# Sixty-eight weight tiles at distances of their own, and every other pair read backward

## The chip, the cores and the metric

The kernel runs on one core of one Trainium2 chip. The metric is the device time of one launch in microseconds (us): 628.13 us before the change, the median of three runs from 628.09 to 628.43. TensorE does the products (PE in the profile, PEld for its weight loads), VectorE (DVE) and ScalarE (ACT) prepare operands and drain results, GpSimd (POOL) and SyncE (SP) mostly issue DMAs.

## The reference

One transformer-like layer on a (512, 1024) input in float32. The change touches the input projection of the gated MLP alone, the second line below:

```python
h = layer_norm(ALPHA * h + mixed @ w_out[l], ln1_g[l], ln1_b[l])
a, u = jnp.split(h @ w_ffn_in[l], 2, axis=-1)      # w_ffn_in: (1024, 2 * 2816)
a = causal_dwconv(a, conv_w[l], conv_b[l])
f = (jax.nn.gelu(a, approximate=False) * u) @ w_ffn_out[l]
h = layer_norm(ALPHA * h + f, ln2_g[l], ln2_b[l])
```

## The kernel before, in words

Everything is kept transposed: channels on the 128 partitions, the 512 tokens along the free dimension. Each float32 operand is split into a high part (`split`, L71: a rounding copy to float32r on ScalarE, L75) and a low part (the rest, on VectorE, L76), and one float32 product is three float32r matmuls, high by high, high by low, low by high (`mm3`, L240, whose matmuls stand on L242, L245 and L246). In each, a 128 x 128 block of weights is loaded as the stationary operand and the activations are the moving operand.

The FFN input has 22 pairs of 128 output channels (one for `a`, one for `u`). Pairs 2 to 18 (`SEVEN`, 17 of them) are computed with Strassen-like products of seven, on blocks of half the channels by half the tokens, so their moving operand has 256 columns. A pair has four combined weight tiles: A, X and Y of 128 x 1024 and D of 128 x 512. `s_mm` (L271) multiplies half a tile (four blocks) with one of the block combinations of h: A twice, X twice, Y twice, D once. So a pair takes 7 x 4 x 3 = 84 matmuls, and the 17 pairs take 1428. Of these 24 fall to each A, X and Y and 12 to each D. The products go into halves of PSUM banks: `ba` and `bc` in `seven_a` (L277), `bb` in `seven` (L284); in the profile their names are saf, scf and sbf (sai and sag and so on for the same scheme in the first projections). The pairs 0, 1 and 19 to 21 are done plainly (`fi_mm`, L879).

The high and low weight tiles live in rings of five slots each (`slot`, L122), tags `whi` and `wlo`. A slot is `SLOT = D + 64` float32 wide, 4352 bytes in a partition, which is 17 x 256. In the built program both rings, and all the wide activation tiles that TensorE reads beside them (hT_hi, hT_lo, the combinations T3, T4, nT1, nT2, xT, zT, sd), start at 192 mod 256 bytes of the partition. So the distance of a weight block from the moving operand, mod 256, is the offset of the tile in its slot: `BESIDE = 2` elements, 8 bytes, for all products of seven and for the four plain tiles of pairs 0 and 1 (`near`), and 0 bytes for all others.

The order of the work on each engine is fixed by a scheduler when the program is built. TensorE runs ahead through banks and slots, and the ring of weight tiles is filled `LEAD = 3` tiles ahead (`weights`, L235; `fetch`, L129; `fetch_seven`, L193, which forms the combined weights and calls `slot` on L207).

Of the kernel before, what the change touches and what calls it, by code (L numbers as in the profile page):

```python
# [34 lines left out]
BESIDE = 2  # L35
# [7 lines left out]
SEVEN = tuple(range(2, 19))  # L43
# [8 lines left out]
def layer_kernel(ctx: ExitStack, tc: tile.TileContext, xT, x, w_v, w_c, rel_bias, invcnt, w_group,  # L52
# [14 lines left out]
    def flip(v):  # L67
        (pst, pn), (_, n) = v.ap
        return bass.AP(tensor=v.tensor, offset=v.offset + P - 1, ap=[[pst, pn], [P, n // P], [-1, P]])

    def split(hi, lo, src, copy=None):  # L71
        if copy:
            copy(hi, src)
        else:
            state["hi"] = nc.scalar.activation(hi, src, AF.Copy)  # L75
        state["lo"] = nc.vector.tensor_tensor(lo, src, hi.bitcast(F32), op=ALU.subtract)  # L76
        return state["lo"]
# [41 lines left out]
    ready = {}  # L119


    def slot(i, n, near=False):  # L122
        o = BESIDE if near else 0
        return tuple(wp.tile([P, SLOT], F32R, tag=f"w{q}", name=f"w{q}{i}", bufs=RING)[:, o:o + n]
                     for q in ("hi", "lo"))

# [2 lines left out]
    def fetch(pool=None, early=None):  # L129
# [17 lines left out]
        if isinstance(chunks[i], tuple):  # L147
            ready[i] = (fetch_fo if i >= FO0 else fetch_seven)(i, *chunks[i])
            return
        raw = wp.tile([P, D], F32, tag="wraw", name=f"wraw{i}", bufs=3)  # L150
        if pool is None:
            hi, lo = slot(i, D, FI0 <= i < FI0 + COVER)
        else:
            hi = pool.tile([P, D], F32R, name=f"whi{i}")
            lo = pool.tile([P, D], F32R, name=f"wlo{i}")
        parts = 2 if early else 1
        for c in range(parts):
            sl = slice(c * (D // parts), (c + 1) * (D // parts))
            (nc.scalar if early else nc.sync).dma_start(raw[:, sl], chunks[i][:, sl])
            split(hi[:, sl], lo[:, sl], raw[:, sl])  # L160
            if c == 0 and early:
                state["w0"] = raw[:, sl]
                early()
# [29 lines left out]
    def fetch_seven(i, key, q):  # L193
        n = S if q == "D" else D
        raw = raws[key, "A" if q == "Y" else q]
        if q == "X" and key in SUMMED:
            with tc.issue_after(state["Y"].ins):
                for c, o in ((slice(S, D), raws[key, "D"]), (slice(0, S), raws[key, "A"][:, :S])):
                    nc.vector.tensor_tensor(raw[:, c], raw[:, :S], o, op=ALU.add)
        if q == "Y":  # L200
            with ExitStack() as held:
                if key == ("f", COVER // 2):
                    held.enter_context(tc.issue_after(state["h"].ins))

                for c, o in ((slice(0, S), raws[key, "X"][:, S:]), (slice(S, D), raw[:, :S])):
                    nc.vector.tensor_tensor(raw[:, c], o, raw[:, c], op=ALU.add)
        hi, lo = slot(i, n, True)  # L207
        state[q] = split(hi, lo, raw)
        return hi, lo

# [6 lines left out]
    def fetch_fo(i, name, c):  # L217
        sl = piece(c)
        n = sl.stop - sl.start
        step = {"T3": "=B11", "B11": "+B12", "T1": "+B22", "T2": "+B21", "T4": None}  # L220
        if name in step:
            raw = tw[:, sl]
        else:
            raw = wp.tile([P, D], F32, tag="wraw", name=f"wraw{i}", bufs=3)[:, :n]
            nc.sync.dma_start(raw, half(name, sl))
        hi, lo = slot(i, n)
        split(hi, lo, raw)
        then = step.get(name)
        if then and then[0] == "+":
            nc.gpsimd.dma_start(raw, half(then[1:], sl), accum_op=ALU.add)  # L230
        elif then:
            nc.sync.dma_start(raw, half(then[1:], sl))
        return hi, lo

    def weights(i):  # L235
        while state["next"] <= min(i + LEAD, state["limit"]):
            fetch()
        return ready[i]

    def mm3(out_, w, a, start, stop, pin=False, **kw):  # L240
        (wh, wl), (ah, al) = w, a
        ins = nc.tensor.matmul(out_, wh, ah, start=start, stop=False, **kw)  # L242
        if pin:
            tc.keep_in_program_order(ins)
        nc.tensor.matmul(out_, wh, al, start=False, stop=False, **kw)  # L245
        nc.tensor.matmul(out_, wl, ah, start=False, stop=stop, **kw)  # L246

    def split3(v, a):
        return tuple(t.rearrange("p (a c) -> p a c", a=a) for t in v)
# [20 lines left out]

    def s_mm(key, q, part, act_, b, start, pin=False):  # L271
        wh, wl = split3(weights(at[(*key, q)]), 4 if q == "D" else KT)
        for k in range(4):
            mm3(b, (wh[:, 4 * part + k, :], wl[:, 4 * part + k, :]), (act_[0][:, k, :], act_[1][:, k, :]),
                start and k == 0, k == 3, pin and k == 0, skip_group_check=not start)

    def seven_a(key, whole, y):  # L277
        ba, bc = (bank(f"s{q}{key[0]}{key[1]}") for q in "ac")
        s_mm(key, "A", 0, (whole[0][:, k1, t1], whole[1][:, k1, t1]), ba[:, 256:], True)
        nc.scalar.activation(y, ba[:, 256:], AF.Copy)  # L280
        s_mm(key, "A", 1, (whole[0][:, k2, t1], whole[1][:, k2, t1]), bc[:, :256], True)
        return ba, bc

    def seven(key, whole, tt, y, u, done, between=None, begun=None):  # L284
        ba, bc = begun or seven_a(key, whole, y)
        bb = bank(f"sb{key[0]}{key[1]}")
        chain, low, c11 = ba[:, 256:], bb[:, :256], bc[:, :256]

        def b_(k, t):
            return whole[0][:, k, t], whole[1][:, k, t]  # L290

        flush()
        s_mm(key, "X", 0, tt["T3"], low, True)
        nc.scalar.activation(u[:, t2], low, AF.Copy)
        s_mm(key, "Y", 0, tt["nT2"], chain, False)
        nc.scalar.activation(u[:, t1], chain, AF.Copy)
        s_mm(key, "D", 0, tt["T4"], low, False)
        nc.vector.tensor_tensor(u[:, t1], u[:, t1], low, op=ALU.add)
        if between:
            between()  # L300
        s_mm(key, "X", 1, tt["nT1"], chain, False, between)
        nc.vector.tensor_tensor(u[:, t2], u[:, t2], chain, op=ALU.add)
        state["add"] = nc.vector.tensor_tensor(ba[:, t1], y, c11, op=ALU.add)

        def close():
            s_mm(key, "Y", 1, b_(k2, t2), chain, False, between)
            done(ba, u)

        pending.append(close)
# [93 lines left out]
    for kt in range(KT):  # L403
        wh, wl = split3(weights(kt // 2), 2)
        wh, wl = wh[:, kt % 2, :], wl[:, kt % 2, :]
# [197 lines left out]
    ap = attn.enter_context(tc.tile_pool(name="ap", bufs=2, reuse_waits="tile"))  # L603
# [72 lines left out]
    def br_mm(f, br, b=None, ks=range(4), pin=False):  # L676
        wh, wl = split3(weights(at["br", f]), KT)
        b = b or bank(f"br{f}_{br}")
        for k in ks:
            src = (zT_hi[:, k, :], zT_lo[:, k, :]) if br else (oT_hi[:, k, :], oT_lo[:, k, :])  # L680
            mm3(b, (wh[:, 4 * br + k, :], wl[:, 4 * br + k, :]), src, k == 0, k == 3, pin and k == ks[0])
        return b
# [7 lines left out]
    for f in range(KT - 1):  # L690
# [4 lines left out]
        for br in (1, 0):  # L695
            b = br_mm(f, br)
            if f < GSEVEN:
                t = gslot[8 * br + f]
                nc.vector.tensor_tensor(t, t, b, op=ALU.mult)
            else:  # L700
                t = branch[f, br] = unused.pop(0)
# [11 lines left out]
    def gate_done(f, ba, u):  # L713
        if f < KT - 1:
            for br, v, scale in ((0, ba, 1.0), (1, u, -1.0)):
                nc.scalar.activation(v, v, AF.Sigmoid, scale=scale)
                nc.vector.tensor_tensor(branch[f, br], branch[f, br], v, op=ALU.mult)
            merged(f, branch[f, 0], branch[f, 1])
        else:
            for br, v, scale in ((0, ba, 1.0), (1, u, -1.0)):  # L720
                gslot[8 * br + f] = unused.pop(0)
                nc.scalar.activation(gslot[8 * br + f], v, AF.Sigmoid, scale=scale)
# [6 lines left out]
    for f in range(GSEVEN, KT):  # L729
        if f == KT - 1:  # L730
# [3 lines left out]
              lambda ba, u, f=f: gate_done(f, ba, u), first_half if f == KT - 1 else None)  # L734
# [427 lines left out]
```

## Time and profile before

| | |
|---|---|
| median of the runs | 628.13 us |
| the profiled execution, from first to last instruction | 625.9 us |
| PE busy | 616.0 us, 98% |
| PEld busy | 552.9 us, 88% |
| DVE busy | 505.2 us, 81% |
| ACT busy | 353.8 us, 57% |

The span is that of one profiled execution, and lies 2.2 us under the median of the runs; times read from the trace are differences within it. In this profile the end of a matmul is modelled and matmuls overlap, so neither the mean duration of one (278 ns for 256 columns) nor the busy share tells how fast they follow each other. That is read from the starts: two rows of the timeline, and the number of matmuls between them.

### The profile page before, as it was taken

How to read it: one execution, taken by the hardware profiler on the slowest of the kernel's cores; microseconds unless marked ns; L12 is line 12 of the kernel's file. 1: busy time of each engine (PE TensorE's matmuls, PEld its weight loads, DVE VectorE, ACT ScalarE, POOL GpSimd, SP SyncE). 2: the span in 40 equal slices, each digit the busy share in tenths (PEclk: the TensorE clock that was granted, in tenths of full speed). 3: DMA queues.
4: the chain of work that ended last, by engine and by line, in shares of the span. 5: the costliest groups of instructions: out<-in, count | busy, mean ns of one | idle time of the engine just before them, and what ended most of it. 6: DMA issues, size and time to landing. Idle time of an engine off the chain costs nothing.

```text
span 625.9 us, 10417 instructions
## 1 busy us (share of the span) xinstructions
PE 616.0 (98%) x3988; PEld 552.9 (88%) x3988; DVE 505.2 (81%) x780; ACT 353.8 (57%) x536; POOL 119.0 (19%) x131
## 2 busy tenths in 40 slices
PE   8999999999999999999999999999999999999994
PEld 6899998777788998889999999999999888888884
DVE  6978787776494788399998988898988869798886
ACT  6646777655644567125566565566656346555442
POOL 0133134323132101110110101101100302123302
PEclk9999999999999999999999999999999999999998
DMA  9566647422548515816668687687745996899805
GB/s 321 163 193 187 177 121 223 134 78 78 169 111 211 149 60 177 293 43 225 146 167 208 184 201 185 176 201 201 187 97 161 325 254 127 221 192 207 195 1 134
DMA packets 40545, 107.70 MB, mean 172 GB/s; under 512 B 4384, under 2 KB 4648, under 8 KB 40240
## 3 DMA queue, kind: packets, MB, share of 16 engines
q1 hardware_dynamic: 27264, 71.90, 34.8%
q0 software_dynamic: 12656, 34.10, 28.0%
q10 hardware_dynamic: 576, 1.05, 0.5%
q8 instruction: 31, 0.51, 0.4%
q14 instruction: 18, 0.15, 0.1%
HBM read 102.82 MB, written 3.17 MB: 169 GB/s over the span
## 4 chain that ended last, share of the span: by engine, by line
PE 98%; DVE 1%; DMA 1%; DVEq 0%; issue 0%
PE saf L242 5%; PE saf L245 5%; PE saf L246 5%; PE v L420 3%; PE fi L242 3%; PE fi L245 3%; PE fi L246 3%; PE sbf L242 3%; PE sbf L246 3%; PE sbf L245 2%; PE br L242 2%; PE g L242 2%; PE g L246 2%; PE g L245 2%; PE wo L242 2%; PE br L246 2%
## 5 line engine op out<-in xcount | busy, mean ns | idle before, releaser
L75 ACT ACTIVATE whi<-wraw 128x1024 fp32r<-128x1024 f32 (+1 forms) x53 | 53.8, 1023 | 39.6 <-DMA wraw<-in_w_fo 8.1
L76 DVE TENSOR_TENSOR wlo<-wraw,whi 128x1024 fp32r<-128x1024 f32 (+1 forms) x53 | 65.1, 1235 | 12.7 <-ACT whi L75 12.5
L76 DVE TENSOR_TENSOR wlo<-araw,whi 128x1024 fp32r<-128x1024 f32 x52 | 63.3, 1225 | 9.4 <-ACT whi L75 9.1
L75 ACT ACTIVATE whi<-araw 128x1024 fp32r<-128x1024 f32 x52 | 54.4, 1058 | 20.2 <-PE saf L245 5.6
L189 POOL DMA_DIRECT2D xraw<-in_w_fi x15 | 18.0, 1203 | 135.9 <-DMA xraw<-in_w_fi 69.2
L75 ACT ACTIVATE whi<-tw 128x1024 fp32r<-128x1024 f32 (+1 forms) x30 | 29.5, 983 | 25.4 <-DMA tw<-in_w_fo 10.7
L76 DVE TENSOR_TENSOR wlo<-tw,whi 128x1024 fp32r<-128x1024 f32 (+1 forms) x30 | 33.5, 1129 | 9.0 <-ACT whi L75 9.0
L242 PE MATMUL sbf<-T_hi,whi 128*128 128x256 f32 x136 | 37.9, 279 | 0.0
L242 PE MATMUL saf<-hT_hi,whi 128*128 128x256 f32 x136 | 37.9, 279 | 0.0
L242 PE MATMUL saf<-nT_hi,whi 128*128 128x256 f32 x136 | 37.8, 278 | 0.0
L245 PE MATMUL saf<-hT_lo,whi 128*128 128x256 f32 x136 | 37.8, 278 | 0.0
L246 PE MATMUL saf<-nT_hi,wlo 128*128 128x256 f32 x136 | 37.8, 278 | 0.0
L246 PE MATMUL sbf<-T_hi,wlo 128*128 128x256 f32 x136 | 37.7, 278 | 0.0
L245 PE MATMUL sbf<-T_lo,whi 128*128 128x256 f32 x136 | 37.7, 277 | 0.0
L245 PE MATMUL saf<-nT_lo,whi 128*128 128x256 f32 x136 | 37.7, 277 | 0.0
L246 PE MATMUL saf<-hT_hi,wlo 128*128 128x256 f32 x136 | 37.6, 277 | 0.0
L245 PE MATMUL fi<-hT_lo,whi 128*128 128x256 f32 (+1 forms) x112 | 36.2, 326 | 0.0
L246 PE MATMUL fi<-hT_hi,wlo 128*128 128x256 f32 (+1 forms) x112 | 36.2, 325 | 0.0
L242 PE MATMUL fi<-hT_hi,whi 128*128 128x256 f32 (+1 forms) x112 | 36.1, 327 | 0.0
L560 POOL TENSOR_SCALAR pp<-pp,rs 128x128 f32<-128x128 f32 (+3 forms) x32 | 25.2, 803 | 36.7 <-DVE rs L557 26.6
L230 POOL DMA_DIRECT2D tw<-in_w_fo x18 | 15.6, 896 | 61.4 <-DVE wlo L76 61.4
L555 ACT ACTIVATE pp<-pp,nm 128x128 f32<-128x128 f32 (+3 forms) x32 | 17.6, 551 | 14.8 <-DVE nm L552 14.8
(346 smaller groups left out, 2171.8 us busy)
## 6 DMA issues: line engine op xcount, KB each, us to landing
tw<-in_w_fo POOLq DMA_DIRECT2D x20, 512.0 KB, 8.1
araw<-in_w_fi SPq DMA_DIRECT2D x17, 512.0 KB, 3.9
xraw<-in_w_fi SPq DMA_DIRECT2D x15, 512.0 KB, 4.3
xraw<-in_w_fi POOLq DMA_DIRECT2D x15, 512.0 KB, 6.2
wraw<-in_w_c SPq DMA_DIRECT2D x10, 512.0 KB, 4.4
wraw<-in_w_fi SPq DMA_DIRECT2D x10, 512.0 KB, 3.7
wraw<-in_w_fo SPq DMA_DIRECT2D x10, 512.0 KB, 5.1
tw<-in_w_fo SPq DMA_DIRECT2D x10, 512.0 KB, 7.5
```

The costliest lines, as they stand in the source:

```text
L75: state["hi"] = nc.scalar.activation(hi, src, AF.Copy)
L76: state["lo"] = nc.vector.tensor_tensor(lo, src, hi.bitcast(F32), op=ALU.subtract)
L189: state["acc"] = nc.gpsimd.dma_start(v, bass.AP(tensor=a.tensor, offset=a.offset, ap=[[pst, pn], [u.offset + S - a.offset, 2], [est, S]]), ...
L230: nc.gpsimd.dma_start(raw, half(then[1:], sl), accum_op=ALU.add)
L242: ins = nc.tensor.matmul(out_, wh, ah, start=start, stop=False, **kw)
L245: nc.tensor.matmul(out_, wh, al, start=False, stop=False, **kw)
L246: nc.tensor.matmul(out_, wl, ah, start=False, stop=stop, **kw)
L420: ins = nc.tensor.matmul(bs[j], xs_[j][a], (wh, wl)[b], start=kt == 0 and n == 0, stop=False)
L555: exps[h] = nc.scalar.activation(pp[:, offs[i]:offs[i] + n], pp[:, offs[i]:offs[i] + n], AF.Exp, bias=nm[:, i:i + 1], accum_out=rs[:, i:i ...
L560: nc.gpsimd.tensor_scalar(pp[:, offs[i]:offs[i] + n], pp[:, offs[i]:offs[i] + n], rs[:, i:i + 1], 1.0, op0=ALU.mult, op1=ALU.mult)
```

## The change

Each of the 68 weight tiles of the 17 pairs gets an offset of its own in its slot (the same in the high and the low ring), in place of 2 elements for all. Among the nine even pairs the 36 tiles get 0, 2, 4 ... 62 elements (0, 8, 16 ... 248 bytes) and the last four 1, 3, 5 and 7 elements (4, 12, 20, 28 bytes); among the eight odd pairs the 32 tiles get 0, 2, 4 ... 62 elements. For the odd pairs the moving operand is read backward, from the last of its 256 columns to the first, and the PSUM output is written backward too, so each result lands where it did. What is computed, and all other tiles, stay as they were.

```diff
+    def back(v):
+        (pst, pn), (_, n) = v.ap
+        return bass.AP(tensor=v.tensor, offset=v.offset + n - 1, ap=[[pst, pn], [-1, n]])
...
+    apart = {}
+    for turned in range(2):
+        tiles = [("f", f, q) for f in SEVEN if f % 2 == turned for q in "AXYD"]
+        apart.update((key, (2 * n if n < 32 else 2 * n - 63) % 64) for n, key in enumerate(tiles))
+
+    def slot(i, n, near=False, o=None):
+        if o is None:
+            o = BESIDE if near else 0
         return tuple(wp.tile([P, SLOT], F32R, tag=f"w{q}", name=f"w{q}{i}", bufs=RING)[:, o:o + n]
                      for q in ("hi", "lo"))
...
-        hi, lo = slot(i, n, True)
+        hi, lo = slot(i, n, True, apart.get((*key, q)))
...
     def s_mm(key, q, part, act_, b, start, pin=False):
         wh, wl = split3(weights(at[(*key, q)]), 4 if q == "D" else KT)
+        turn = back if key[0] == "f" and key[1] % 2 else lambda v: v
         for k in range(4):
-            mm3(b, (wh[:, 4 * part + k, :], wl[:, 4 * part + k, :]), (act_[0][:, k, :], act_[1][:, k, :]),
+            mm3(turn(b), (wh[:, 4 * part + k, :], wl[:, 4 * part + k, :]), tuple(turn(t[:, k, :]) for t in act_),
                 start and k == 0, k == 3, pin and k == 0, skip_group_check=not start)
```

Built, the two programs hold the same instructions in the same order on all five engines, and every tile has the same place. Beside the operands, only waits for a semaphore of TensorE's own differ, at seven matmuls: six first matmuls into `bc` (scf) of odd pairs get one, and one into `bb` (sbf) of pair 5 loses it. The first of the six, on TensorE in pair 5, stands here with its wait, first before the change and then after it (saf is `ba`, scf is `bc`, the numbers are those of single tiles):

```order
L246 MATMUL saf_3443<-hT_hi,wlo_3448 128x256
L242 MATMUL saf_3691<-hT_hi,whi_3625 128x256 [waits Activation_49]
L245 MATMUL saf_3691<-hT_lo,whi_3625 128x256
L242 MATMUL scf_3692<-hT_hi,whi_3625 128x256
L245 MATMUL scf_3692<-hT_lo,whi_3625 128x256
L246 MATMUL saf_3567<-nT_hi,wlo_3572 128x256 [waits DVE_49]
```

```order
L256 MATMUL saf_3443<-hT_hi,wlo_3448 128x256
L252 MATMUL saf_3691<-hT_hi,whi_3625 128x256 [waits Activation_49]
L255 MATMUL saf_3691<-hT_lo,whi_3625 128x256
L252 MATMUL scf_3692<-hT_hi,whi_3625 128x256 [waits PE_49]
L255 MATMUL scf_3692<-hT_lo,whi_3625 128x256
L256 MATMUL saf_3567<-nT_hi,wlo_3572 128x256 [waits DVE_49]
```

The instructions stand in the same order; the fourth has a wait more.

## Rows read from the trace of the kernel before

**Rows 1.** The page: busy time of each engine, TensorE's granted clock by slices

```profile
PE 616.0 (98%) x3988; PEld 552.9 (88%) x3988; DVE 505.2 (81%) x780; ACT 353.8 (57%) x536; POOL 119.0 (19%) x131
...
PEclk9999999999999999999999999999999999999998
```

**Rows 2.** The chain of waits, 429.9 to 432 us: start, us, what

```profile
429.94 0.11 PE saf L246
430.06 0.12 PE saf L242
430.17 0.12 PE saf L245
...
431.10 0.12 PE scf L242
```

**Rows 3.** Windows: stretch, its us, busy of each engine, clock, DMA

```profile
317.23:472.54 155.31, 155.31 (x1347) 155.31 (x1346) 137.65 (x197) 96.76 (x145) 18.05 (x15) 1.00 0.71 180
```

**Rows 4.** Groups by line and shape, TensorE: count, busy, mean ns

```profile
L242 PE MATMUL sbf<-T_hi,whi 128*128 128x256 f32 x136 | 37.9, 279 | 0.0
...
L242 PE MATMUL scf<-hT_hi,whi 128*128 128x256 f32 x68 | 19.0, 279 | 0.0
```

**Rows 5.** Timeline of PE, products of seven of the FFN

```profile
317.23 0.28 PE L242 MATMUL sbf<-T_hi,whi 128*128 128x256 f32 x1
...
472.54 0.28 PE L242 MATMUL saf<-nT_hi,whi 128*128 128x256 f32 x1
```

**Rows 6.** Timeline of PE, last product of the FFN output, distance 0

```profile
612.72 0.28 PE L242 MATMUL fo_cut<-whi,sd_hi 128*128 128x256 f32 x1
...
617.16 0.28 PE L245 MATMUL fo_cut<-wlo,sd_hi 128*128 128x256 f32 x1
```

**Rows 7.** Timeline of PE, plain FFN pairs, 512 columns, distance 0

```profile
507.66 0.39 PE L245 MATMUL fi<-hT_lo,whi 128*128 128x512 f32 x1
...
511.96 0.39 PE L246 MATMUL fi<-hT_hi,wlo 128*128 128x512 f32 x1
```

**Rows 8.** The chain of waits at transposes of 128 columns

```profile
99.81 0.87 PE tr L615 x8
277.99 1.75 PE ht L845 x16
```

**Rows 9.** Groups by line and shape, ACT and DVE, weight splits

```profile
L75 ACT ACTIVATE whi<-araw 128x1024 fp32r<-128x1024 f32 x52 | 54.4, 1058 | 20.2 <-PE saf L245 5.6 <-PE scf L245 3.5 <-PE sai L245 2.6
L75 ACT ACTIVATE whi<-tw 128x1024 fp32r<-128x1024 f32 x25 | 26.3, 1054 | 20.4 <-DMA tw<-in_w_fo 10.7 <-PE fod L246 5.9 <-PE fob L246 1.9
L76 DVE TENSOR_TENSOR wlo<-araw,whi 128x1024 fp32r<-128x1024 f32 x52 | 63.3, 1225 | 9.4 <-ACT whi L75 9.1
L76 DVE TENSOR_TENSOR wlo<-tw,whi 128x1024 fp32r<-128x1024 f32 x25 | 30.3, 1220 | 9.0 <-ACT whi L75 9.0
```

**Rows 10.** The same view: PSUM read backward (PT) and forward (vv, gates)

```profile
L617 ACT ACTIVATE PT<-tr 128x512 f32<-128x512 f32 x8 | 4.8, 595 | 2.6 <-PE tr L615 2.5
L411 ACT ACTIVATE vv<-v 128x512 f32<-128x512 f32 x4 | 2.2, 597 | 2.4 <-PE v L246 2.4
L618 DVE COPY PT<-tr 128x512 f32<-128x512 f32 x8 | 5.5, 686 | 1.1 <-PE tr L615 1.0
L494 DVE COPY gates<-g 128x512 f32<-128x512 f32 x8 | 5.5, 682 | 6.0 <-PE g L246 5.9
```

**Rows 11.** Timeline of PE, a matmul that waits for TensorE's own semaphore

```profile
317.11 0.28 PE L246 MATMUL fi<-hT_hi,wlo 128*128 128x256 f32 x1
...
317.35 0.28 PE L245 MATMUL sbf<-T_lo,whi 128*128 128x256 f32 x1
```

More of the change, by code (lines that the diff above doesn't have):

```diff
@@ L119, in layer_kernel @@
     ready = {}
-    def slot(i, n, near=False):
-        o = BESIDE if near else 0
+    apart = {}
[5 more added lines that the diff above has]
+            o = BESIDE if near else 0
         return tuple(wp.tile([P, SLOT], F32R, tag=f"w{q}", name=f"w{q}{i}", bufs=RING)[:, o:o + n]
```

## The prediction

> **What bounds the kernel now.** The page comes first: TensorE is busy for 98% of the span and its granted clock is full, the 2.4 GHz level, in all slices but the last [rows 1]. The chain of waits then shows what kind of bound this is: through the FFN stage it is matmul after matmul, each a step of 0.11 to 0.12 us, with no other engine between [rows 2]. The window over the products of seven says the same: PE is busy for 155.31 of 155.31 us at clock 1.00, VectorE for 137.65 and ScalarE for 96.76 [rows 3]. So nothing that is late for TensorE matters there; what counts is how fast one matmul may follow another. The mean of 278 to 279 ns in the groups is a modelled length and no step [rows 4]. The step is read from starts. From 317.23 to 472.54 us TensorE starts 1344 matmuls of products of seven: 155.31 us / 1344 = 115.6 ns [rows 5]. Streaming 256 columns at 2.4 GHz takes 106.7 ns, so 8.9 ns of each step is something else.
>
> What else it is shows where only the distance differs. In the last product of the FFN output the moving operand again has 256 columns, but weights and moving operand lie at distance 0 mod 256: 37 steps in 4.44 us, 120.0 ns [rows 6]. The plain FFN pairs at distance 0 have 512 columns: 19 steps in 4.30 us, 226.3 ns, against 213.3 ns of streaming [rows 7]. So at distance 0 a matmul pays 13 ns over its columns, whatever their number, and at 8 bytes it pays 8.9. The cost hangs on the load, of which there is one per matmul in both, and on how its addresses stand to those of the operand streaming at the time. A stage with cheaper pairs yet are the transposes: a 128-column load each, and 16 in 1.75 us, 109.4 ns (8 in 0.87 us, 108.8 ns) [rows 8]; there the moving operand runs more slowly, 0.85 ns a column. So loads alone can follow each other every 109 ns.
>
> **The change part by part.** No instruction is added, removed or moved. What changes is the step of 1428 matmuls: 9 even pairs x 84 = 756 read forward, 8 odd pairs x 84 = 672 read backward. Each nanosecond on the mean step is 1.43 us on the chain, and all of it ends up in the time, since TensorE is never idle in the stage [rows 3] and what follows it hangs on it.
>
> Distances, forward. The trace knows two: 120.0 ns at 0 and 115.6 ns at 8 bytes. The change uses every multiple of 8 from 0 to 248 once and four odd multiples of 4. The cheap end is the 109.4 ns of the transposes, if some distance lets load and stream never meet: 6.2 ns less. The dear end of what was measured is 120.0: 4.4 ns more. The two known places differ by half a 16-byte step, and I take it that this is what they differ by: half of the distances (0, 16, 32 ... 240) are then like 0 and half (8, 24 ... 248) like 8, with the four odd ones between. The mean is 117.8 ns, 2.2 ns more: 756 x 2.2 = +1.7 us. Keeping both ends: 756 x (-6.2 to +4.4) = -4.7 to +3.3 us.
>
> Backward. No matmul of this kernel reads its operand or writes PSUM with a step of -1. On the other engines reading PSUM backward in blocks of 128 costs nothing: 595 ns against 597 ns forward on ScalarE, 686 against 682 on VectorE [rows 10]. So I take the backward stream as a stream of the same speed that meets the loads about as often, 117.8 ns again: 672 x 2.2 = +1.5 us. The cheap end is again 109.4 ns (-4.2 us), as the two streams pass each other quickly where they run in opposite directions. The dear end is half speed, by the 0.85 ns a column of the transposes [rows 8]: 256 columns in 218 ns, 672 x 102.4 = +69 us; this end is far from the rows of reading backward, so it enters as a rival and not in the value.
>
> Splits into the shifted slots. ScalarE writes a high tile at offset 8 bytes in 1058 ns and at offset 0 in 1054, VectorE a low tile in 1225 and 1220 [rows 9]; 4 and 5 ns on 68 tiles, on engines with 18 and 59 us free in the window [rows 3], cost nothing. If the steps fell to 109 ns, VectorE's share would go from 89% to 94%, still enough.
>
> The seven waits that differ. TensorE waits for an own matmul of more than fifty earlier. In the kernel before, the first matmul of pair 2 into sbf has such a wait and stands 0.12 us behind its predecessor and 0.12 us ahead of its successor [rows 5, 11]: nothing.
>
> The sum: 625.9 + 1.7 + 1.5 = 629.1 us for the profiled span; the runs before lie 2.2 us above theirs, so 628.1 + 3.2 = 631.3 us.
>
> Two rules of the Trainium skill speak on this. In "SBUF — State Buffer", section "Who interferes with whom", PE has two independent read ports, one for the moving operand and one for weight loads, and "PE and ACT never wait on anyone"; by that no distance would matter and the time stay at 628.1. The trace does not agree, with 115.6 ns at one distance and 120.0 at another [rows 5, 6]. In "Advanced Engine Details and Errata", section "PSUM Cachelines", any non-contiguous pattern in PSUM slows matmuls significantly, while two neighbours in a line are best; whether a step of -1 counts as contiguous it does not say, and no run here shows it yet. It would speak for the half-speed rival below.
>
> **The rivals.**
> - Only coinciding places are dear. The cost comes where the streams start at the same place mod 256, so 0 is the exception and every other distance costs 115.6, in both directions. For it: 0 costs half as much again as 8 over the columns (13.3 against 8.9 ns). Against: 8 bytes still pays 8.9 ns. Two tiles of 24 matmuls at 0: 48 x 4.4 = +0.2 us, 628.3 us: no change.
> - 8 is the exception. All other distances cost what 0 costs, or more, forward and backward: 1380 x 4.4 = +6.1 us, 634.2 us: slower. For it: all stages at 0 pay the same 13 ns with quite different tiles. Against: nothing but that a place next to a bad one would hardly be the one good one.
> - Most places are free, or the opposite direction is. A step of 109.4 ns in one of the two directions, the other unchanged: 672 or 756 x 6.2 = -4.2 to -4.7 us, about 623.7 us: faster. In both, 628.1 - 8.9 = 619.2. For it: the transposes show that loads can follow at 109 ns [rows 8], and 0 and 8 lie side by side in a range of 256 of which the rest is unseen. Against: in the transposes the stream is slower, so the load has more room. It decides as soon as the mean over all tiles falls below 115.6.
> - Backward runs at half speed, 628.1 + 69 = 697 us.
>
> **How the numbers follow.** Half and half (631.3 us) 0.38; only 0 dear (628.3) 0.20; 8 the exception (634.2) 0.18; free places (623.7, at most 619.2) 0.20; half speed 0.04. A change of 0.2%, 1.3 us or 0.9 ns on the mean step, is about what can be told from none. Slower takes the first, third and last, less a little for a mean that ends inside 0.9 ns: 0.58. Same is the second and that little: 0.21. Faster: 0.21. The range reaches from 623.0, which takes in one direction free, to 636.0, which takes in the 634.2 and some distances dearer than 0; what is left out is both directions free and half speed. The likeliest case alone runs from 629.5 to 633.
>
> **What would show it.** In the profile after, the starts of the matmuls of each product give its step: forward tiles at multiples of 16 bytes near 120 ns and those between near 115.6 bear out the value taken; 115.6 nearly everywhere, 120 nearly everywhere, or steps toward 109 each name a rival. The odd pairs show the same for the backward stream by themselves. The window from pair 2's first sbf to the first plain 512-column matmul should be 158 to 159 us long in place of 155.3, with PE busy throughout. Splits on L75 and L76 (ten lines later after the change) should keep their means. The forecast is wrong if steps differ by more than 16-byte position, above all if forward and backward part company, or if TensorE shows idle time in the stage.

## The result, and the profile after

The changed kernel takes 632.10 us (median of 3 runs, 632.03 to 632.72) where the kernel before takes 628.13: a ratio of 1.0064, with an interval of 1.0045 to 1.0084. It is slower, by 4.0 us. The profiled execution of it took 632.72 us, with a span of 631.0.

The page of the kernel after, busy time and TensorE's granted clock, answers to [rows 1]:

```profile
PE 621.2 (98%) x3988; PEld 557.6 (88%) x3988; DVE 505.2 (80%) x780; ACT 354.5 (56%) x536; POOL 118.6 (19%) x131
...
PEclk9999999999999999999999999999999999999997
```

TensorE has the same 3988 matmuls at the same full clock and is busy for 5.2 us more; the other engines stand within 0.7 us of where they were. The window over the products of seven answers to [rows 3]: stretch, its length, busy time and count of PE, PEld, DVE, ACT and POOL, clock, DMA share, GB/s.

```profile
318.24:477.48 159.24, 159.24 (x1347) 159.24 (x1346) 138.07 (x197) 97.26 (x145) 18.05 (x15) 1.00 0.70 175
```

It runs between the same two matmuls as before, pair 2's first into sbf and the first into saf that comes 1344 matmuls later. It was 155.31 us long and is 159.24, still without idle time on PE: 118.5 ns a step in place of 115.6. The whole of the loss in this window, 3.93 us, is in how fast one matmul follows another. The other 1.2 us of span lie outside it. Before the window 1.0 us is lost, of which the first tile of pair 2 (now at distance 0) accounts for about 0.1 us, and 0.9 us had gone by TensorE's hundredth matmul, 26 us into the span, among instructions that are the same in both; runs of this one kernel differ by 0.7 us.

The chain of waits (start, us, what) answers to [rows 2]: still matmul after matmul with no other engine between, each 0.11 to 0.12 us, here where pair 13 goes on to sbf.

```profile
430.43 0.12 PE saf L252
430.54 0.12 PE saf L255
430.66 0.12 PE saf L256
430.78 0.12 PE sbf L252
```

The steps differ from product to product. The timeline of TensorE after, answering to [rows 5] (start, length, engine, line, operation, out<-in), shows one product each at distance 8 forward, 64 forward, 72 backward and 216 forward (in pairs 2, 6, 7 and 14):

```profile
318.24 0.28 PE L252 MATMUL sbf<-T_hi,whi 128*128 128x256 f32 x1
...
319.63 0.28 PE L252 MATMUL saf<-nT_hi,whi 128*128 128x256 f32 x1
...
353.96 0.28 PE L256 MATMUL scf<-hT_hi,wlo 128*128 128x256 f32 x1
...
355.10 0.28 PE L252 MATMUL sbf<-T_hi,whi 128*128 128x256 f32 x1
...
366.49 0.28 PE L252 MATMUL sbf<-T_hi,whi 128*128 128x256 f32 x1
...
367.93 0.28 PE L252 MATMUL saf<-nT_hi,whi 128*128 128x256 f32 x1
...
440.53 0.28 PE L252 MATMUL sbf<-T_hi,whi 128*128 128x256 f32 x1
...
441.85 0.28 PE L256 MATMUL sbf<-T_hi,wlo 128*128 128x256 f32 x1
```

At 8 there are 12 steps in 1.39 us, 115.8 ns; at 64 10 steps in 1.14 us, 114.0; at 72 read backward 12 in 1.44, 120.0; at 216 11 in 1.32, 120.0. So 64 runs below the 115.6 ns of before, and 216, an odd multiple of 8 as 8 itself is, runs at the 120 ns of distance 0.

Summed over all 1428 matmuls that were changed, start to start, the steps take 169.29 us; in the kernel before it is 165.12. The even pairs went from 115.70 to 118.35 ns (756 matmuls), the odd ones from 115.56 to 118.78 (672). The weight splits into the shifted slots, in groups by line and shape (count, busy us, mean ns, idle before), answer to [rows 9]:

```profile
L79 ACT ACTIVATE whi<-araw 128x1024 fp32r<-128x1024 f32 x52 | 54.4, 1058 | 21.1 <-PE saf L255 6.5 <-PE scf L255 4.3 <-PE sai L255 2.6
L80 DVE TENSOR_TENSOR wlo<-araw,whi 128x1024 fp32r<-128x1024 f32 x52 | 63.2, 1223 | 9.8 <-ACT whi L79 9.5
```

1058 ns as before, and 1223 for 1225: where in the slot a tile lies costs these engines nothing.

### The profile page after: what moved, and what is told of

Its sections match the earlier page's. It is cut to its first block, busy times and chain, and to the rows that moved or that the text cites. A ratio compares the mean times of both kernels' runs of the same rounds, so it can differ in the third digit from the quotient of the medians.

```text
span 631.0 us, 10417 instructions
## 1 busy us (share of the span) xinstructions
PE 621.2 (98%) x3988; PEld 557.6 (88%) x3988; DVE 505.2 (80%) x780; ACT 354.5 (56%) x536; POOL 118.6 (19%) x131
## 4 chain that ended last, share of the span: by engine, by line
PE 98%; DVE 1%; DMA 1%; DVEq 0%; issue 0%
PE saf L255 5%; PE saf L252 5%; PE saf L256 5%; PE v L431 3%; PE fi L252 3%; PE fi L256 3%; PE fi L255 3%; PE sbf L252 3%; PE sbf L255 3%; PE sbf L256 3%; PE br L252 2%; PE g L252 2%; PE g L256 2%; PE g L255 2%; PE wo L255 2%; PE br L255 2%
## 5 line engine op out<-in xcount | busy, mean ns | idle before, releaser
L79 ACT ACTIVATE whi<-wraw 128x1024 fp32r<-128x1024 f32 (+1 forms) x53 | 53.9, 1023 | 39.8 <-PE g L255 6.2
L80 DVE TENSOR_TENSOR wlo<-wraw,whi 128x1024 fp32r<-128x1024 f32 (+1 forms) x53 | 65.1, 1235 | 12.3 <-ACT whi L79 12.1
L80 DVE TENSOR_TENSOR wlo<-araw,whi 128x1024 fp32r<-128x1024 f32 x52 | 63.2, 1223 | 9.8 <-ACT whi L79 9.5
L79 ACT ACTIVATE whi<-araw 128x1024 fp32r<-128x1024 f32 x52 | 54.4, 1058 | 21.1 <-PE saf L255 6.5
L79 ACT ACTIVATE whi<-tw 128x1024 fp32r<-128x1024 f32 (+1 forms) x30 | 29.5, 983 | 25.0 <-DMA tw<-in_w_fo 10.5
L80 DVE TENSOR_TENSOR wlo<-tw,whi 128x1024 fp32r<-128x1024 f32 (+1 forms) x30 | 33.4, 1126 | 8.4 <-ACT whi L79 8.4
L255 PEld LDWEIGHTS saf<-hT_lo,whi 128*128 128x128 f32 x136 | 25.6, 188 | 0.0
```

## The experiments

What they had to settle: is it the distances or the direction, is it the distance or the weight's place alone, and what kind of rule leads from a distance to a step. Experiments 1 and 2 start from the changed kernel, the others from the kernel before, read forward throughout; in those with offsets of their own `slot` has the parameter `o` of the change. Line numbers move by a few lines from run to run. Rows are rounded to 0.01 us, so a step read over ten matmuls is good to about 1 ns. Steps below are from start to start, over the products of seven of the FFN; "the window" is the one of 1344 matmuls above. The kernel before, run beside them, took 627.67, 628.04 and 628.00 us on the three chips (experiments 1 to 4, 5 to 7, 8 to 10).

**1. The distances alone, all pairs forward.** From the changed kernel:

```diff
-        turn = back if key[0] == "f" and key[1] % 2 else lambda v: v
+        turn = lambda v: v
```

> The changed kernel with every pair read forward; the 68 distances stay. Theory D (the distance of a tile sets its step, the direction matters little): the odd pairs' mean step goes from 118.8 ns to about the 118.3 ns that the even pairs have over the same places, 672 x -0.5 = -0.3 us, 631.8 us. Rival B (reading backward is what costs in the odd pairs): their step falls to the 115.6 ns of before, 672 x -3.2 = -2.1 us, 630.0 us.

Measured: 631.75 us, ratio 1.0060 (1.0044 to 1.0075). The odd pairs, now forward, step at 117.90 ns where they took 118.78 backward; the even pairs, unchanged, at 118.30. So of the 4.17 us the distances make 2.0 (even) + 1.6 (odd), and reading backward adds 672 x 0.88 ns = 0.6 us. These are one trace of each kernel, and single tiles moved between them without any change of their own: the tile at 64 of pair 6, forward in both, has a mean step of 114.8 ns in the changed kernel and 117.6 here. So not all of the 0.6 us need be the direction's.

The trace of this run holds something else. Two products lie at the same distance, 192, both forward (TensorE's timeline, pairs 14 and 15, 24 steps from the first row to the second in each):

```profile
432.19 0.28 PE L252 MATMUL saf<-hT_hi,whi 128*128 128x256 f32 x1
...
434.91 0.28 PE L252 MATMUL sbf<-T_hi,whi 128*128 128x256 f32 x1
...
442.02 0.28 PE L252 MATMUL saf<-hT_hi,whi 128*128 128x256 f32 x1
...
444.85 0.28 PE L252 MATMUL sbf<-T_hi,whi 128*128 128x256 f32 x1
```

2.72 us and 2.83 us: 113.3 ns and 117.9 ns at one distance. A distance doesn't give one step; it has several settled rhythms. (A rhythm is a step, or a short pattern of steps, that matmuls keep up from one to the next.)

**2. Backward alone, at distance 8.** The odd pairs read backward, every tile at 8 bytes as in the kernel before:

```diff
-        hi, lo = slot(i, n, True, apart.get((*key, q)))
+        hi, lo = slot(i, n, True)
```

> The kernel before with the odd pairs read backward, all tiles at 8 bytes. Theory D (every place has a step of its own in each direction): the odd pairs go at the 119.7 ns that the one tile at 8 bytes showed backward, 672 x +4.1 = +2.7 us, 630.8 us. Rival H (the cost is that distances change from tile to tile, so that loads and stream never settle): with one distance throughout nothing is lost, 115.6 ns, 628.1 us.

Measured: 630.84 us, ratio 1.0050 (1.0033 to 1.0067). Backward steps are 119.58 ns, forward ones 116.30. TensorE's timeline of a product read backward, pair 3:

```profile
325.56 0.28 PE L252 MATMUL sbf<-T_hi,whi 128*128 128x256 f32 x1
...
327.00 0.28 PE L252 MATMUL saf<-nT_hi,whi 128*128 128x256 f32 x1
```

12 steps in 1.44 us, 120.0 ns, against 115.6 forward. So backward is dearer by 4.4 ns here and by 0.9 ns on the mean over the distances of experiment 1: the price is not one of the direction alone, it changes with the distance. Rival H falls, since one distance throughout still lost 3.2 us.

**3. All tiles of the FFN at 64.** 64 bytes had run below 115.6 ns in one product of the changed kernel, 114.0 by the rows above:

```diff
-        hi, lo = slot(i, n, True)
+        hi, lo = slot(i, n, True, 16 if key[0] == "f" else None)
```

> The kernel before with all 68 tiles of the 17 pairs at 64 bytes in place of 8, read forward. Theory D: the step is the 113.4 ns to which the A tile at 64 bytes settled in the changed kernel, 1428 x -2.2 = -3.1 us, 625.0 us. Rival H: any single distance settles to the same 115.6 ns, 628.1 us.

Measured: 624.56 us, ratio 0.9948 (0.9933 to 0.9963): faster than the kernel before. The window:

```profile
317.17:469.52 152.35, 152.35 (x1346) 152.35 (x1345) 137.34 (x196) 96.56 (x145) 18.05 (x15) 1.00 0.71 183
```

152.35 us / 1344 = 113.4 ns, over the whole window. Rival H falls again: a single distance need not give 115.6.

**4. The moving operands moved in place of the weights.** The tile at the edge of the right side grows from 32 to 96 bytes, so the operands made there shift by 64; weights of the FFN lie at offset 0.

```diff
-    edge.tile([P, 8], F32, name="edge_t")
+    edge.tile([P, 24], F32, name="edge_t")
...
-        hi, lo = slot(i, n, True)
+        hi, lo = slot(i, n, True, 0 if key[0] == "f" else None)
```

> The kernel before with all 68 tiles at offset 0 of their slots, and the tiles on the right side of SBUF 64 bytes lower, so that the block combinations (T3, nT2, T4, nT1) lie 64 bytes below the weights mod 256 while hT stays at distance 0. Theory D (the distance counts, not the address of the weights): products on hT take 120.0 ns, those on the combinations 113.4 ns, with the same tiles X and Y giving both. Rival A (the address of the weight tile by itself, or its alignment, counts): both take 120.0 ns, as weights at offset 0 do in the kernel before. By the same theory D the plain first projections (512 columns on xT, now at distance 64) should take less than their 226.7 ns, about 220.

Measured: 632.38 us (one run). Every weight tile of the stage lies at the same place, but hT has stayed (distance 0) and the combinations T and nT have moved (distance 64). TensorE's timeline, first 9 steps of a product on T, then 10 steps of one on hT:

```profile
339.17 0.28 PE L243 MATMUL sbf<-T_hi,whi 128*128 128x256 f32 x1
...
340.19 0.28 PE L243 MATMUL saf<-nT_hi,whi 128*128 128x256 f32 x1
...
340.88 0.28 PE L246 MATMUL saf<-hT_lo,whi 128*128 128x256 f32 x1
...
342.08 0.28 PE L243 MATMUL scf<-hT_hi,whi 128*128 128x256 f32 x1
```

113.3 ns and 120.0 ns. Over the whole stage the 816 matmuls on T and nT average 114.8 ns (115.6 before) and the 612 on hT 119.0 (115.7 before). So with the weights in one place the step goes by where the moving operand lies, and with the moving operand in one place it went by where the weights lie (experiment 3): what counts is the distance, not the weight's place. The total is no gain. The stage itself loses 1.4 us, -0.6 on T and nT and +2.0 on hT, whose distance went from 8 to 0. And the moved edge also put the 512-column products on xT at distance 64: there a settled step took 233 ns in place of about 227 (1.3 us on the 240 matmuls of p and g), which the expectation had put at 220. A distance that is good for 256 columns is bad for 512.

**5. All 256-column products at 64**, those of the earlier stages too:

```diff
-BESIDE = 2
+BESIDE = 16
```

> The kernel before with BESIDE = 16: every tile that is multiplied with 256 columns (the products of seven of all three stages and the plain tiles of pairs 0 and 1) lies at 64 bytes in place of 8. Theory D with rhythms (a distance sets which rhythms a run of matmuls can settle to; at 64 there are two, 113.4 and 117.8 ns): mostly 113.4 ns, on 1428 + 420 + 336 + 192 matmuls 2.2 ns less each, 5.2 us less than before, 622.5 us on the scale of the chip that gave 627.7. Rival: outside the FFN the runs are cut by waits too often to settle, so only the 3.1 us of the FFN come, 624.6 us.

Measured: 632.78 us, ratio 1.0052 (1.0026 to 1.0078). Neither theory expected a loss. Eight executions fall in two groups: 627.51 and 627.75, and six between 632.44 and 633.30; even the shorter two lie 5 us above the 622.5 expected. In the profiled one (633.23) the window is long:

```profile
319.91:478.20 158.29, 158.29 (x1346) 158.29 (x1345) 138.03 (x197) 97.09 (x145) 18.05 (x15) 1.00 0.69 176
```

That is 117.8 ns at a distance that gave 113.4 in experiment 3. Its timeline on TensorE shows where it ends:

```profile
477.14 0.28 PE L242 MATMUL sbf<-T_hi,whi 128*128 128x256 f32 x1
...
478.20 0.28 PE L242 MATMUL saf<-nT_hi,whi 128*128 128x256 f32 x1
...
478.44 0.40 PE L242 MATMUL fi<-hT_hi,whi 128*128 128x512 f32 x1
478.67 0.40 PE L245 MATMUL fi<-hT_lo,whi 128*128 128x512 f32 x1
...
479.02 0.28 PE L242 MATMUL saf<-nT_hi,whi 128*128 128x256 f32 x1
...
481.06 0.28 PE L242 MATMUL saf<-hT_hi,whi 128*128 128x256 f32 x1
```

9 steps in 1.06 us, 117.8 ns; two matmuls of 512 columns; then 18 steps in 2.04 us, 113.3 ns, at the same distance. Here the rhythm held for the whole window at one distance, and was another after two matmuls of another shape. Only this execution, one of the longer six, was traced. That the two shorter ones ran the stage at 113.3 ns is not shown; it fits the gap of 5 to 6 us between the groups, as the window here is 5.9 us longer than in experiment 3.

**6. 512 columns at other distances.** 24 plain tiles at multiples of 8 bytes that are no multiples of 32:

```diff
-            hi, lo = slot(i, D, FI0 <= i < FI0 + COVER)
+            hi, lo = slot(i, D, FI0 <= i < FI0 + COVER, plain.get(i))
```

(where `plain` deals out the offsets; FFN as before)

> The kernel before with the 24 weight tiles that are multiplied with 512 columns (p, g, br and the FFN pairs 19 to 21) at 24 distances of their own, the multiples of 8 bytes that are no multiples of 32. Theory D: 512 columns have a curve of their own, and since 64 bytes took 233 ns where 0 takes 226.7, most places lie between, mean about 230 ns, 576 x 3.3 = +1.9 us; some place may lie below 226.7. Rival (0 is simply the good place for a long stream): every place is over 228 ns, mean 231 or more, +2.5 us or more.

Measured: 630.53 us (one run). Of the distances tried none beat 0, which has 226.7 ns in the same trace: the means by tile are mostly 231 to 233.5 ns, the lowest 228.1 (at 120). TensorE's timeline of one of the plain pairs, 19 steps, answers to [rows 7]:

```profile
510.17 0.40 PE L246 MATMUL fi<-hT_hi,whi 128*128 128x512 f32 x1
...
514.60 0.40 PE L249 MATMUL fi<-hT_lo,whi 128*128 128x512 f32 x1
```

4.43 us, 233.2 ns a step against 226.3.

**7. One distance per pair, 32 to 96 in steps of 4 bytes:**

```diff
-        hi, lo = slot(i, n, True)
+        hi, lo = slot(i, n, True, 8 + key[1] - SEVEN[0] if key[0] == "f" else None)
```

> The kernel before with one distance for each pair of the FFN's products of seven, 32 to 96 bytes in steps of 4 (pair 10 has 64), read forward. Theory D with rhythms: 64 bytes alone settles at 113.4 ns, its neighbours at 4 and 8 bytes are no better than 117 to 119 as 56 and 72 were, mean over the stage about 118 ns, +3.4 us. Rival (the good place is a band some 16 bytes wide around 64): 56 to 72 all settle near 113.4, mean about 117, +1.9 us.

Measured: 630.56 us (one run), mean step 117.82 ns. There is no band around 64, and 64 is not alone. By pair: 84 bytes gives 120.0 ns, and 36 settles there too (119.3 on the mean); 48 gives 117.7, or 117 and 130 by turns; 60 about 119.5; 32, 40, 44, 56, 68, 72, 80, 92 and 96 lie between 117.8 and 119.3; 64 has products at 113.3 and others at 117.8. 76 and 88, and mostly 52, run into 113.3 in nearly every product. TensorE's timeline of 26 steps at 76:

```profile
423.10 0.28 PE L247 MATMUL saf<-hT_hi,wlo 128*128 128x256 f32 x1
...
426.04 0.28 PE L243 MATMUL saf<-nT_hi,whi 128*128 128x256 f32 x1
```

2.94 us, 113.1 ns, which is 113.3 within the rounding of the rows.

**8. All tiles of the FFN at 76**, as experiment 3 but for the offset:

```diff
-        hi, lo = slot(i, n, True, 16 if key[0] == "f" else None)
+        hi, lo = slot(i, n, True, 19 if key[0] == "f" else None)
```

> The kernel before with all 68 tiles of the 17 pairs at 76 bytes, read forward. Theory R (a distance has one or more settled rhythms; at 76 every product that was seen ran into 113.3 ns, whatever it came from): 1428 x -2.3 = -3.2 us, 624.8 us where before takes 628.0, and all executions alike. Rival C (no distance holds: with all tiles at one place another, slow rhythm shows, as at 64): executions at two times, some of them at 628 or above.

Measured: 625.04 us, ratio 0.9952 (0.9939 to 0.9966), 113.4 ns in the window. As good as 64.

**9. All 256-column products at 76**, as experiment 5 but for the offset:

```diff
-BESIDE = 16
+BESIDE = 19
```

> The kernel before with BESIDE = 19: every tile that is multiplied with 256 columns at 76 bytes, in all three stages. Theory R: 113.3 ns on 1428 + 420 + 336 + 192 matmuls, less some restarts in the first projections, -4.8 us, 623.2 us where before takes 628.0. Rival C: as at 64, two groups of executions, the slow one above 628 us.

Measured: 623.60 us (5 runs, 622.70 to 623.79), ratio 0.9927 (0.9914 to 0.9939): the lowest median of all, ahead of both kernels, and in these five executions without experiment 5's two groups. The window:

```profile
316.30:468.62 152.32, 152.32 (x1347) 152.32 (x1345) 137.58 (x196) 96.74 (x145) 18.05 (x15) 1.00 0.71 184
```

**10. All at 64 again, but the stage entered from 8.** As experiment 5, only that the four plain tiles whose 256-column products come right before and among the first of the FFN stage lie at 8 bytes:

```diff
-        o = BESIDE if near else 0
+        o = (2 if FI0 <= i < FI0 + COVER else BESIDE) if near else 0
```

> The kernel with everything of 256 columns at 64 bytes, but the four plain tiles of pairs 0 and 1, from which the FFN's products of seven are entered, back at 8. Theory R (the rhythm that a stretch has at 64 is the one it was entered with, and lasts until something breaks it): the FFN stage runs at 113.5 ns as with the first projections at 8, -3.1 us there, while the first projections stay at 117.8, +1.6 us: about 626.5 us. Rival (what made everything at 64 slow was the first projections or the sum of things, not the entry): the FFN stage stays at 117.7 ns, 632 us.

Measured: 626.43 us, ratio 0.9981 (0.9961 to 1.0001); nine of ten executions between 625.80 and 627.59, one at 632.79. In the profiled one the FFN stage runs at 113.4 ns, while the earlier 256-column products at 64, which are entered as in experiment 5, run at 117.6 to 117.8:

```profile
319.11:471.43 152.32, 152.32 (x1346) 152.32 (x1345) 137.39 (x196) 96.70 (x145) 18.05 (x15) 1.00 0.71 183
```

Same tiles, same distance, same order in this window as in experiment 5; only what runs ahead of it and between its first products differs, and the window is 6 us shorter. One distance, two rhythms, and the way in shifts which of them comes: nine of ten executions take the shorter time with an entry from 8, two of eight with one from 64. The two kernels ran on different chips, which this comparison leaves as a rival; each chip showed both groups of times.

## Why the prediction was right, and where its reasoning was not

The forecast of 631.3 us stands against 632.1. Its steps:

- **The bound.** Right. TensorE is never idle in the window before or after, and the time moves by the sum of the steps: 4.17 us on 1428 matmuls, 4.0 us on the time. What hides elsewhere stays hidden: the splits cost nothing, VectorE is busy for 138.07 of 159.24 us. The experiments bear it out in the other direction: 113.4 ns a step brought the time 3.1 us under the kernel before (experiment 3).
- **The cause, load against stream by their distance.** That the distance counts is right, shown by experiments 3 and 4 together: weights that stay in place step at 113.3 or 120.0 ns by where the moving operand lies. That it is load and stream meeting that costs the time is argued and not shown. The Trainium skill, "SBUF — State Buffer", section "Who interferes with whom", gives PE two independent read ports, one for the moving operand and one for weight loads; if that is to mean that neither operand's place matters to the other, these runs do not agree, with 113.3 to 120.0 ns for one matmul and nothing changed but addresses. And "13 ns over its columns, whatever their number", read at distance 0, is no rule for other distances: at 64 bytes a matmul of 256 columns takes less than at 0 (113.3 against 120.0 ns) and one of 512 columns more (233 against 226.7).
- **Distances, forward: +1.7 us.** Measured 756 x (118.35 - 115.70) = +2.0. The size was near, and the step by which it came was wrong: "the two known places differ by half a 16-byte step, and I take it that this is what they differ by". By that, forward tiles at multiples of 16 should take 120.0 and odd multiples of 8 115.6. They take 118.41 and 118.31, and the odd multiples of 4 118.2. The rule isn't there, and by the prediction's own sign ("wrong if steps differ by more than 16-byte position") this step of it failed. The mean came out near by luck: its two levels, 115.6 and 120.0, happen to have their middle (117.8) close to where most distances lie.
- **Backward: +1.5 us.** Measured 672 x (118.78 - 115.56) = +2.2, of which the distance alone makes 1.6 (experiment 1) and the direction some 0.6, by one trace of each kernel. The value taken rests on the same rule of half a 16-byte step, so its nearness is luck too. That the backward stream has the same speed was right: no half speed. The Trainium skill's "Advanced Engine Details and Errata", section "PSUM Cachelines", has matmuls slowed significantly by non-contiguous patterns in PSUM; a step of -1 costs 0.9 ns on the mean and 4.4 at distance 8, and even there the 120.0 ns is the level of distance 0 forward, so by these runs a step of -1 does not slow matmuls significantly. That it "meets the loads about as often" held on the mean, not at distance 8, where experiment 2 alone loses 3.2 us.
- **The splits and the seven waits.** 1058 and 1223 ns in the splits, and no idle time on PE in the window; nothing, as forecast. (The splits stand four lines later, on L79 and L80, not ten.)
- **The rivals.** "Only coinciding places are dear" fell: at most distances the step is over 115.6. "8 is the exception" was the nearer one; 8 is a good place among mostly worse ones, but those lie at 118.6 ns on the mean and not at 120. "Most places are free" fell, but its grain of truth is what experiments 3, 8 and 9 use: some distances run at 113.3. The low end of 109.4, taken from the transposes, was reached nowhere.

Two things stay open. Why a distance has the rhythms that it has isn't shown by any run here: the traces give steps, not where load and stream meet. And 76 may have a slower rhythm that no run has fallen into; the times of experiments 8 and 9, 5 executions each, lie within 1.3 us and show none.

## What to carry to other kernels

Where TensorE is never idle and each matmul has a load of its own, measure the step from start to start for each product, not the mean length in the groups, and try one distance between weights and moving operand for a whole stage rather than a spread of them: here the spread got a mean of 118.5 ns, and one good distance got 113.3. What is good depends on the number of columns (of the distances tried here, 0 was the best for 512 and among the dearest for 256), and two points of such a curve give no law for the rest. Run a chosen distance several times, since one distance can have two rhythms, and its first profile shows only one of them.

## What the runs showed of the hardware that was not expected

- Steps of a 256-column matmul with its own load settled here on a few levels, 113.3, 115.6, 117.8 and 120.0 ns, or alternated around 118 to 119. Distance 8 forward settled at 115.6 (before, and in the longer forward stretches of experiment 2), 216 at 120.0 (after, and experiment 1), 64 at 113.3 or 117.8, 76 at 113.3.
- A rhythm is kept across products at one distance, and what went ahead seems to bear on which it is; one trace of each kernel shows it, and both kernels have executions of the other group. In experiments 5 and 10, the stage's first product at 64 follows the same transposes; in the one it settles at 117.8 and in the other at 113.3, from its second step on. TensorE's timeline of experiment 5, 9 steps of that product:

```profile
306.13 0.28 PE L242 MATMUL saf<-hT_hi,whi 128*128 128x256 f32 x1
...
307.19 0.28 PE L242 MATMUL scf<-hT_hi,whi 128*128 128x256 f32 x1
```

and of experiment 10, the same 9 steps:

```profile
305.64 0.28 PE L242 MATMUL saf<-hT_hi,whi 128*128 128x256 f32 x1
...
306.66 0.28 PE L242 MATMUL scf<-hT_hi,whi 128*128 128x256 f32 x1
```

1.06 us against 1.02: 117.8 and 113.3 ns for the same instructions at the same addresses, after products at 64 and at 8.

- The executions of one kernel can fall in two groups at the same granted clock: 627.5 to 627.8 us and 632.4 to 633.3 in experiment 5, all at 0.996 to 0.997. With all these operands at 76 in place of 64 (experiment 9) five executions showed one group. That the two rhythms make the two groups is likely by the sizes, and not shown.
